# Projection steps of a hybrid S5 / delta-rule encoder given to the scheduler with high priority

## The chip, the cores and the metric

The kernel runs on one core of one Trainium2 chip. The metric is the device time of one execution in microseconds, the median of three runs.

## What is computed

One encoder block in float32 on a sequence of 512 tokens of width 1024. The input is normalized and projected by `w_in` to a stream u for an S5 scan (width 512), to q, k, v, z for a gated delta rule with 4 heads of 128 (512 each), and to the gates beta and a. Cut to what matters:

```
h = rmsnorm(x); u, q, k, v, z, beta, a = split(h @ w_in)
y = s5_scan(u, forward) + s5_scan(u, backward)          # 32 groups of 16 channels, 64 states
q, k, v = silu(conv5(q, k, v)); q, k = l2norm(q), l2norm(k)
o = chunked_delta(q, k, v, g, beta) + flip(chunked_delta(flipped))   # chunks of 64
mix = concat(s5 output, norm(o) * silu(z)) @ w_out + x
x2 = mix + cross_attention(mix, mem)                     # memory of 256 rows
out = x2 + mixture_of_experts(x2)                        # 4 x 8 experts, 2 chosen
```

## The kernel before

`build` (L1510 on) issues the work stage by stage in Python. A scheduler then lists the instructions of each engine: it runs a timeline of its own and takes, of those that are ready, the one with the highest priority, by default the one that was issued first. On the chip every engine works through its list strictly in order. So the order in which `build` issues steps, and any priority that it gives them, set the lists.

The stages around the change, in the order of the program:

- `stage_a` normalizes and transposes x into `ht` (8 blocks of 128 by 512 tokens). `proj_u` makes four projections by `proj` (L179: one 512 KB weight load `wst` through SP's queue, four buffers, then eight matmuls of 128x512 in `mm8`, L143, into one of two banks). `gates` makes the decays; it ends with nine small copies on DVE (L579 to L598: gc, sdl, sbe, csr, cso), between which ACT loads a table for exp (L580).
- `gdn_in` (L614) makes the 12 blocks k0, q0, k1, q1, ..., k3, q3, v0 to v3. Each: a projection, two copies out of its bank by ACT (xp L636, cv L637), two small memsets of xp on POOL (L633, L634), four taps on DVE (L639), silu on ACT (L640), four transposes (L648); for q and k also squares, a power on POOL (L666), a scaling and four more transposes (L673). Its pool reuses the memory of the gates, so the first xp waits for the last of the gates' copies.
- `s5_params` (L232 on) makes the S5 tables in eight steps. Each makes `pm` and `ca` by a complex multiply of six 128x512 operations (L225 to L230) on DVE or POOL, by two lists of eight entries (`PM_ENG`, `CA_ENG`), writes `ca` to memory, transposes `pm` (L372), copies it (`bct`, L373), multiplies `bb` by `ca` (L381), copies the result (`wl`, L387 on), writes it to `w_scr`, and multiplies `bct` by the transposed u (L404). `pm`, `ca` and `bct` have one buffer each.
- `weave` advances several generators in turn in proportion to given counts; here it interleaves the 13 steps of `gdn_in` with the 9 of `s5_params` (L1556).
- Next, woven again: `gdn_inv` (the matrix N of the delta rule in four blocks, L698 to L726, a series of 31 steps on DVE, its products L768 to L778), four z projections and eight memory blocks `mem_kv` (128x256 matmuls, also L143), and the recurrence `s5_rec` on DVE. Then `gdn_chain` (eight dependent steps, PE at L834 to L851) with the other eight memory blocks; then the output of the S5 scan (`tz`, L446, read back from `w_scr`), the mixing, the cross attention, and the experts, whose weights stream in to the end.

Of the kernel before, what the change touches and what calls it, by code (L numbers as in the profile page):

```python
# [43 lines left out]
def weave(*streams):  # L44

    live = [[g, n, 0] for g, n in streams]
    while live:
        s = min(live, key=lambda t: (t[2] + 0.5) / t[1])
        s[2] += 1
        if next(s[0], s) is s:  # L50
            live.remove(s)


CA_ENG = (1, 1, 0, 1, 1, 1, 0, 1)
# [3 lines left out]
class Enc:  # L58
# [1448 lines left out]
    def build(self):  # L1507
        nc, tc, ctx, A = self.nc, self.tc, self.ctx, self.A
# [40 lines left out]
        with tc.tile_pool(name="gi", bufs=2) as gi:  # L1549
            qkv = self.gdn_in([(w, n, h) for h in range(4) for w, n in ((1, "k"), (0, "q"))] +  # L1550
                              [(2, "v", h) for h in range(4)], gi)
            s5 = self.s5_params()
            next(s5)
            for _ in u:
                pass
            weave((qkv, 13), (s5, 9))  # L1556

        self.gp2 = pool(left, "gp2")
        self.gp3 = pool(left, "gp3")
# [7 lines left out]

        inv = self.gdn_inv()
        weave((inv, 16), (rest(), 13), (itertools.islice(rec, 16), 17))
        gv.close()  # L1570
        r2.close()
        self.set_banks(ch=(3, 4, 5, 6, 7), out=(2,), tp=(1,), mm=(0,))
        weave((self.gdn_chain(), 20), (kv, 9), (rec, 47))
        r1.close()

# [202 lines left out]
```

## Time and profile before

| | us |
|---|---|
| three runs | 893.8, 893.03, 889.67 (median 893.03) |
| the profiled execution | 892.26 |
| its span | 890.5 |
| PE busy | 783.1 (88%) |
| DVE busy | 404.3 (45%) |
| ACT busy | 329.4 (37%) |
| POOL busy | 232.6 (26%) |

PE is TensorE's matmuls, PEld its weight loads, DVE VectorE, ACT ScalarE, POOL GpSimd, SP SyncE, whose queue carries most of the transfers. Start times count from the start of the span. A matmul of 128x512 in float32 shows as two records. PEclk is the granted TensorE clock as a share of full speed, so 0.50 is the lower of its two levels (1.2 GHz) and 1.00 the upper (2.4 GHz). A bracket at the end of a row is the idle time of the engine ahead of it, and what ended it.

### The profile page before, as it was taken

What the parts mean: (1) busy time and instruction counts of PE and PEld (TensorE: products, weight loads), DVE (VectorE), ACT (ScalarE), POOL (GpSimd) and SP (SyncE); (2) the same over time, 40 slices, a digit from 0 to 9 for tenths busy, and PEclk for the clock granted to TensorE, in tenths of its full rate; (3) what the DMA queues carried; (4) which work ended last, traced back from release to release, by engine and by line L of the source; (5) the groups of instructions that cost most, each with busy time, mean ns of one, the idle gap of its engine ahead of it and who ended that gap; (6) DMA issues with size and microseconds to landing.
All of it is one profiled execution on the core that took longest, in us unless ns stands there. A gap on an engine that the chain in (4) does not pass through costs nothing. (4 is left out here: it accounts for less than half of the span.)

```text
span 890.5 us, 12981 instructions
## 1 busy us (share of the span) xinstructions
PE 783.1 (88%) x4735; PEld 492.2 (55%) x4736; DVE 404.3 (45%) x1044; ACT 329.4 (37%) x760; POOL 232.6 (26%) x237
## 2 busy tenths in 40 slices
PE   5986998998997997899899999996698878788983
PEld 3443554555586875676688879895333333333331
DVE  4288767678899522244643554324210000000375
ACT  4242454455413235465343464333232131312204
POOL 1022857832100111205161332241311011100103
PEclk9996998999997998999999999998799999999997
DMA  7837222322663308615663714595699999999982
GB/s 206 144 91 111 74 78 74 100 76 98 225 193 104 108 24 169 116 56 172 184 224 96 260 49 159 194 406 187 248 391 412 414 411 408 395 391 410 410 350 102
DMA packets 128130, 185.17 MB, mean 208 GB/s; under 512 B 38734, under 2 KB 93006, under 8 KB 123968
## 3 DMA queue, kind: packets, MB, share of 16 engines
q1 hardware_dynamic: 122736, 172.31, 57.6%
q0 software_dynamic: 5328, 12.01, 3.6%
q8 instruction: 38, 0.62, 0.3%
q14 instruction: 28, 0.23, 0.1%
HBM read 165.50 MB, written 26.18 MB: 215 GB/s over the span
## 5 line engine op out<-in xcount | busy, mean ns | idle before, releaser
L143 PE MATMUL bank<-ht,wst 128*128 128x512 f32 x320 | 151.3, 621 | 4.2 <-ACT kd L583 2.4
L1340 PE MATMUL bank<-mw,xt 128*64 128x512 f32 x360 | 104.5, 595 | 1.5 <-DMA mw<-in_moe_w_up_dram 1.5
L143 PEld LDWEIGHTS bank<-ht,wst 128*128 128x128 f32 x320 | 60.7, 198 | 73.4 <-issue 68.3
L1344 DVE SCALAR_TENSOR_TENSOR hs<-hs,tw,bank 128x256 f32<-128x256 f32 x16 | 7.7, 480 | 168.9 <-ACT hs L1343 168.9
L1343 ACT ACTIVATE hs<-bank,tw 128x256 f32<-128x256 f32 x16 | 7.6, 474 | 155.5 <-PE bank L1340 155.5
L1380 PE MATMUL bank<-mw,hT 128*64 128x512 f32 x152 | 50.6, 660 | 16.2 <-ACT yd L1385 16.2
L1340 PEld LDWEIGHTS bank<-mw,xt 128*64 128x64 f32 x360 | 33.5, 138 | 55.6 <-issue 52.4
L143 PE MATMUL bank<-mt,wst 128*128 128x256 f32 x256 | 59.9, 393 | 0.0
L639 DVE SCALAR_TENSOR_TENSOR cv<-xp,taps,cv 128x512 f32<-128x512 f32 x48 | 50.4, 1049 | 20.8 <-ACT cv L637 19.7
L972 POOL TENSOR_TENSOR wlo<-wst,whi 128x1024 fp32r<-128x1024 f32 x16 | 38.6, 2416 | 78.7 <-ACT whi L971 78.7
L143 PEld LDWEIGHTS bank<-mt,wst 128*128 128x128 f32 x256 | 50.0, 198 | 7.7 <-issue 0.6
L1320 POOL DMA_INDIRECT xg<-t_scr,tidx x16 | 16.5, 1029 | 136.4 <-PE bank L1327 133.4
L824 POOL TENSOR_TENSOR kt<-kn,kd 64x512 f32<-64x512 f32 x14 | 14.5, 1035 | 97.6 <-PE bank L778 49.8
L1330 ACT ACTIVATE xt<-bank,gm 128x128 f32<-128x128 f32 x128 | 34.7, 382 | 8.9 <-PE bank L1327 7.8
L149 PE MATMUL bank<-wlo,oh 128*128 128x256 f32 x128 | 36.6, 289 | 0.0
L854 DVE SCALAR_TENSOR_TENSOR S<-S,egl,bank 128x128 f32<-128x128 f32 x48 | 15.5, 345 | 46.1 <-PE bank L851 46.1
L150 PE MATMUL bank<-whi,oh 128*128 128x256 f32 x128 | 35.8, 283 | 0.0
L1380 PEld LDWEIGHTS bank<-mw,hT 128*64 128x64 f32 x152 | 14.0, 148 | 38.7 <-issue 20.8
L151 PE MATMUL bank<-whi,ol 128*128 128x256 f32 x128 | 35.3, 287 | 0.0
L149 PE MATMUL bank<-mlo,mxh 128*128 128x512 f32 x64 | 25.8, 405 | 0.8 <-DVE gss L484 0.8
L903 POOL TENSOR_TENSOR mlo<-mst,mhi 128x512 fp32r<-128x512 f32 x16 | 22.0, 1393 | 14.8 <-ACT mhi L902 14.2
L150 PE MATMUL bank<-mhi,mxh 128*128 128x512 f32 x64 | 25.7, 402 | 0.0
(551 smaller groups left out, 1826.3 us busy)
## 6 DMA issues: line engine op xcount, KB each, us to landing
mw<-in_moe_w_down_dram SPq DMA_DIRECT2D x23, 1024.0 KB, 14.7
mw<-in_moe_w_gate_dram SPq DMA_DIRECT2D x45, 512.0 KB, 8.3
mw<-in_moe_w_up_dram SPq DMA_DIRECT2D x45, 512.0 KB, 13.9
wst<-in_w_in_dram SPq DMA_DIRECT2D x20, 512.0 KB, 4.5
ca_scr<-ca SPq DMA_DIRECT2D x8, 512.0 KB, 2.7
wst<-in_xa_wk_dram SPq DMA_DIRECT2D x8, 512.0 KB, 4.3
y_scr<-lhc SPq DMA_DIRECT2D x2, 2048.0 KB
wst<-in_xa_wv_dram SPq DMA_DIRECT2D x8, 512.0 KB, 4.3
```

Of the source, the lines that this page charges most:

```text
L143: self.nc.tensor.matmul(ps, w[:, k, :], act[:, k, :], start=(k == 0), stop=(k == 7))
L149: self.nc.tensor.matmul(ps, ah, bl, start=(first and i == 0), stop=False)
L150: self.nc.tensor.matmul(ps, ah, bh, start=False, stop=False)
L151: self.nc.tensor.matmul(ps, al, bh, start=False, stop=(last and i == n - 1))
L639: v.scalar_tensor_tensor(cv, xp[:, w:w + T], taps[:, w, m:m + 1], cv, op0=OP.mult, op1=OP.add)
L854: v.scalar_tensor_tensor(sn, S[di, h], self.egl[:, ch % 2, ch // 2, di * 4 + h:di * 4 + h + 1], p, op0=OP.mult, op1=OP.add)
L903: nc.gpsimd.tensor_tensor(lo[:, k], st, hi[:, k].bitcast(F32), op=OP.subtract)
L972: nc.gpsimd.tensor_tensor(lo, st, hi.bitcast(F32), op=OP.subtract)
L1320: self.gather = g_.indirect_dma_start(out=xg, out_offset=None, in_=self.t_scr, in_offset=bass.IndirectOffsetOnAxis(ap=self.tidx[:, q:q + 1 ...
L1330: nc.scalar.activation(xt[:, k], ps[:, (k % 4) * P:(k % 4 + 1) * P], AF.Copy, scale=self.gm[:, k:k + 1])
L1340: nc.tensor.matmul(pg[w * 64:w * 64 + 64].rearrange("p (a n) -> p a n", a=2), xt[:, k, w * 64:w * 64 + 64], un[k // 4 * 2 + w][:, :, k % 4 ...
L1380: nc.tensor.matmul(py[w * 64:w * 64 + 64], hT[:, k, w * 64:w * 64 + 64], wd[w][:, k, c], start=(k == 0), stop=(k == 1))
```

## The change

A generator `ahead` passes on the steps of another one, each inside the scheduler's high priority; `build` wraps `gdn_in` in it. Everything below moves down by nine lines. Nothing is computed otherwise than before.

```diff
+def ahead(tc, g):
+
+    while True:
+        with tc.high_priority():
+            if next(g, g) is g:
+                return
+        yield
...
-            weave((qkv, 13), (s5, 9))
+            weave((ahead(tc, qkv), 13), (s5, 9))
```

The lists of the engines change by this. Three places:

**PE, from the last matmul of the gates to the first S5 table.** Banks 571 and 585 are the last two u projections, 607 is k0, 715 q0, 832 k1; `pm` is the first table. Before:

```order
L578 MATMUL bank_280<-g,hfm 128x32 x2
L125 MATMUL bank_357<-ident,U 128x128 x2
L143 MATMUL bank_585<-ht,wst 128x512 x2
L143 MATMUL bank_607<-ht,wst 128x512 x8
L125 MATMUL bank_365<-ident,U 128x128 x2
L143 MATMUL bank_715<-ht,wst 128x512 x2
L125 MATMUL bank_353<-ident,U 128x128 x2
L143 MATMUL bank_715<-ht,wst 128x512 x3
L372 MATMUL bank_656<-ident,pm 128x128 x4
L372 MATMUL bank_662<-ident,pm 128x128 x4
```

Now:

```order
L152 MATMUL bank_607<-ht,wst 128x512 x8
L587 MATMUL bank_280<-g,hfm 128x32
L134 MATMUL bank_357<-ident,U 128x128 x2
L152 MATMUL bank_585<-ht,wst 128x512 x2
L381 MATMUL bank_656<-ident,pm 128x128 x4
L381 MATMUL bank_662<-ident,pm 128x128 x4
L390 MATMUL bank_686<-ca,bb 32x128
L134 MATMUL bank_365<-ident,U 128x128 x2
L390 MATMUL bank_686<-ca,bb 32x128 x5
L134 MATMUL bank_353<-ident,U 128x128 x2
L390 MATMUL bank_686<-ca,bb 32x128 x2
L152 MATMUL bank_832<-ht,wst 128x512 x8
```

k0 still stands ahead of the first table; the five matmuls of q0 that did now stand behind it, and behind the eight of k1 (832), which come first.

**DVE, at the end of the gates.** `b` is an input of `pm`; P are the partial products. Before:

```order
L579 COPY gc<-bank_280 128x32
L228 TENSOR_TENSOR b_392<-b_392,d_560 128x512
L230 TENSOR_TENSOR b_392<-b_392,d_561 128x512
L582 TENSOR_TENSOR sdl<-bank_280,gc 128x32
L589 SCALAR_TENSOR_TENSOR sbe<-beta,egc 128x16
L594 TENSOR_SCALAR csr<-egc 64x4x4
L597 COPY cso<-egc 64x4x4
```

Now:

```order
L357 MEMSET dd 128x128
L234 TENSOR_TENSOR P_637<-aF,b_392 128x512
L235 TENSOR_TENSOR P_638<-aF,b_392 128x512
L236 TENSOR_TENSOR pm<-aF,b_392 128x512
L238 TENSOR_TENSOR pm<-aF,b_392 128x512
L359 TENSOR_TENSOR dd<-ident,dT 16x128 x4
L237 TENSOR_TENSOR pm<-pm,P_637 128x512
L239 TENSOR_TENSOR pm<-pm,P_638 128x512
L234 TENSOR_TENSOR P_754<-aF,b_392 128x512
L235 TENSOR_TENSOR P_755<-aF,b_392 128x512
L588 COPY gc<-bank_280 128x32
L591 TENSOR_TENSOR sdl<-bank_280,gc 128x32
```

The first `pm` and two products of the second now stand ahead of the gates' copies, which stood ahead of it.

**PE, at the first two of the four blocks of N.** Banks 1750 and 1817 hold their differences, 1771 and 1838 the products of k and q; 1801, 1868, 1935 and 2006 are the z projections, 1641 and 1660 belong to tables. Before:

```order
L716 MATMUL bank_1771<-kT 64x64
L717 MATMUL bank_1771<-qT,kT 64x64
L143 MATMUL bank_1801<-ht,wst 128x512 x8
L703 MATMUL bank_1817<-lef,g 64x64 x8
L703 MATMUL bank_1817<-geb,g 64x64 x7
L648 MATMUL bank_1719<-ident,cv 128x128 x4
```

Now, ahead of the first block, and between the first and the second:

```order
L390 MATMUL bank_1660<-ca,bb 32x128 x2
L152 MATMUL bank_1935<-ht,wst 128x512 x6
L152 MATMUL bank_2006<-ht,wst 128x512 x3
L413 MATMUL bank_1641<-uperm,bct 64x64 x14
L712 MATMUL bank_1750<-lef,g 64x64 x8
L712 MATMUL bank_1750<-geb,g 64x64 x8
```

```order
L725 MATMUL bank_1771<-kT 64x64
L726 MATMUL bank_1771<-qT,kT 64x64
L712 MATMUL bank_1817<-lef,g 64x64 x8
L712 MATMUL bank_1817<-geb,g 64x64 x8
L725 MATMUL bank_1838<-kT 64x64
L726 MATMUL bank_1838<-qT,kT 64x64
```

Before, one z projection of eight matmuls stood behind each block of N. Now 27 of their 32 matmuls stand ahead of the first block, four in the third, and one behind the last. The memory blocks behind them move up: 11 instead of 9 stand ahead of the products of the series (L768 before), 12 are done by the first step of the chain where 11 were, and when the last is done 5 steps of the chain are, where 7 were.

## Rows read from the trace of the kernel before

**Rows 1.** Busy time by stretch. Columns: the stretch in us and its length; then busy us (and instructions) of PE, PEld, DVE, ACT and POOL; the granted clock PEclk; the busy share of the DMA engines; GB/s.

```profile
67.44:74.84 7.40, 0.01 (x1) 0.03 (x1) 7.28 (x11) 2.82 (x4) 5.61 (x8) 0.78 1.39 101
74.84:82.80 7.96, 7.96 (x31) 4.25 (x32) 7.89 (x15) 1.97 (x4) 0.14 (x2) 0.50 0.57 141
143.72:154.50 10.78, 10.78 (x35) 4.42 (x36) 9.09 (x12) 5.69 (x18) 6.28 (x7) 0.70 0.13 50
202.53:245.57 43.04, 40.59 (x334) 23.42 (x334) 37.07 (x142) 21.41 (x27) 9.10 (x5) 0.96 0.49 169
245.57:280.68 35.11, 29.30 (x136) 25.49 (x135) 35.03 (x153) 3.08 (x9) 1.28 (x1) 0.99 0.62 185
280.68:301.82 21.14, 21.14 (x293) 19.11 (x294) 16.08 (x54) 9.72 (x18) 4.10 (x4) 0.70 0.18 53
301.82:331.10 29.28, 28.97 (x186) 23.70 (x185) 8.13 (x34) 9.27 (x31) 2.07 (x2) 1.00 0.19 59
400.00:616.30 216.30, 211.06 (x1245) 175.82 (x1244) 89.59 (x168) 92.34 (x179) 69.49 (x46) 0.99 0.57 199
641.50:890.40 248.90, 205.76 (x936) 81.60 (x936) 49.38 (x82) 63.76 (x191) 38.58 (x42) 0.95 0.94 373
```

**Rows 2.** The timeline of PE, from the last projections ahead of the tables. Columns: start in us, busy us of the group, engine, line, operation, out<-in, tile, shape, type, records, and in brackets the idle time ahead of it with what ended it.

```profile
62.66 1.98 PE L143 MATMUL bank<-ht,wst 128*128 128x512 f32 x4 [2.35 <-ACT kd L583]
64.70 2.74 PE L143 MATMUL bank<-ht,wst 128*128 128x512 f32 x6
74.84 1.94 PE L372 MATMUL bank<-ident,pm 128*128 128x128 f32 x8 [7.39 <-DVE pm L228]
78.46 0.69 PE L125 MATMUL bank<-ident,U 128*128 128x128 f32 x2
79.09 1.08 PE L381 MATMUL bank<-ca,bb 64*32 64x128 f32 x10
...
143.72 0.63 PE L381 MATMUL bank<-ca,bb 64*32 64x128 f32 x2 [4.03 <-POOL xp L634]
```

**Rows 3.** The timeline of DVE at the same place, same columns.

```profile
59.90 0.18 DVE L579 COPY gc<-bank 128x32 f32<-128x32 f32 x1
...
60.60 0.68 DVE L230 TENSOR_TENSOR b<-b,d 128x512 f32<-128x512 f32 x1
...
66.24 0.69 DVE L225 TENSOR_TENSOR P<-aF,b 128x512 f32<-128x512 f32 x1
...
67.45 0.34 DVE L593 COPY csr<-sbe 64x16 f32<-64x16 f32 x2
...
68.44 1.75 DVE L229 TENSOR_TENSOR pm<-aF,b 128x512 f32<-128x512 f32 x1
70.11 3.86 DVE L350 TENSOR_TENSOR dd<-ident,dT 16x128 f32<-16x128 f32 x4
74.00 0.69 DVE L228 TENSOR_TENSOR pm<-pm,P 128x512 f32<-128x512 f32 x1
```

**Rows 4.** The timeline of POOL at the same place: the first and the second half of the first `ca`.

```profile
61.58 1.11 POOL L225 TENSOR_TENSOR P<-aR,ct 128x512 f32<-128x512 f32 x1 [5.45 <-issue]
...
68.07 1.57 POOL L228 TENSOR_TENSOR ca<-ca,P 128x512 f32<-128x512 f32 x1
```

**Rows 5.** The timeline of ACT at the same place: the table load of the gates, and the copies out of k0's bank.

```profile
60.15 1.28 ACT L580 ACT_TABLE_LOAD   x1 [4.61 <-DVE gc L579]
...
68.75 0.68 ACT L637 ACTIVATE cv<-bank,taps 128x512 f32<-128x512 f32 x1
```

**Rows 6.** The timeline of PE from the blocks of N to the products of the series.

```profile
202.53 0.68 PE L703 MATMUL bank<-lef,g 128*64 128x64 f32 x16
...
236.66 7.13 PE L143 MATMUL bank<-ht,wst 128*128 128x512 f32 x16
243.63 31.24 PE L143 MATMUL bank<-mt,wst 128*128 128x256 f32 x144
280.68 6.82 PE L768 MATMUL bank<-XT,N 32*32 32x32 f32 x128 [5.81 <-issue]
...
296.67 5.31 PE L143 MATMUL bank<-mt,wst 128*128 128x256 f32 x16
```

**Rows 7.** The timeline of DVE at the last block of N and at the start of the series.

```profile
239.91 0.68 DVE L707 TENSOR_TENSOR e<-bank,gc 128x512 f32<-128x512 f32 x1
...
243.23 1.62 DVE L720 SCALAR_TENSOR_TENSOR N<-bank,beta,e 128x64 f32<-128x64 f32 x8 [1.20 <-ACT e L710]
244.77 0.74 DVE L724 TENSOR_TENSOR qkd<-bank,e 128x256 f32<-128x256 f32 x2
...
245.57 1.97 DVE L731 STREAM_TRANSPOSE NT<-N 128x1024 f32<-128x1024 f32 x1
```

**Rows 8.** The timeline of PE in the chain: its first step, two products of one late step and the next, and the first product of the S5 output.

```profile
301.82 0.38 PE L840 MATMUL bank<-vc,lhc 128*128 128x128 f32 x2
...
333.18 0.49 PE L840 MATMUL bank<-r,lhc 128*128 128x128 f32 x2
...
335.38 0.49 PE L840 MATMUL bank<-r,lhc 128*128 128x128 f32 x2
...
347.45 0.66 PE L446 MATMUL bank<-tz,uperm 128*64 128x128 f32 x2 [4.67 <-DMA tz<-w_scr]
```

**Rows 9.** The page's list of DMA issues: KB each, and the median us from issue to landing.

```profile
wst<-in_w_in_dram SPq DMA_DIRECT2D x20, 512.0 KB, 4.5
```

## The prediction

> **What bounds the kernel now.** I read the page's busy shares first, then the busy time by stretch, then the timelines of PE and of the engines that it waits for. PE is the most used engine, and by stretch two regimes are to be seen. From 641.5 us on, the transfers of the experts' weights bind: their share is 0.94, while PE is busy 205.8 of 248.9 us. From 400 to 616 us PE is busy 211 of 216 us [rows 1]. Ahead of the experts PE is the bound, so time saved on PE before 400 us passes to the end one for one, because the routing, and with it the experts' weights, starts that much earlier. What can be saved is PE's idle time and what it runs at the lower clock. Around the change the timeline of PE shows three such places: 2.35 and 7.39 us ahead of the first table, the second of them put down to DVE's `pm`; 4.03 us ahead of a `ca` product at 143.72 us [rows 2]; 5.81 us at the end of the series [rows 6]. After the first of them the granted clock is 0.50 from 74.84 to 82.80, after the second it is 0.70 over 10.78 us [rows 1].
>
> A second limit lies in the series of 31 steps: DVE is busy 35.03 of 35.11 us there, and PE fills it with 9 memory blocks (144 records) and then waits [rows 1, 6]. Work that is put ahead of the N blocks delays that series; work that is kept for it is hidden.
>
> **The change, part by part.** The arithmetic stays, so each term is a move. The sum runs to the first product of the S5 output, and what follows is taken as unchanged.
>
> *The start.* Before, the gates' copies stood on DVE between `b` (done at 61.28) and the first product P (66.24); the useful `pm` was done at 74.69 and PE went on at 74.84 [rows 2, 3]. Now P follows `b`. Five multiplies and the four `dd` stand ahead of PE. Where POOL is idle a multiply takes 0.69; beside POOL's `ca` one took 1.75, and the four `dd` 3.86 [rows 3, 4]. All at 0.69: 61.3 + 3.5 + 3.9 = 68.6; all at 1.75: 61.3 + 8.75 + 3.86 = 73.9. POOL starts `ca` at 61.58 and had 5.45 us of waiting ahead of it [rows 4], so only the first P is ahead of it: 61.3 + 0.69 + 7.0 + 3.86 = 72.8, and I take that. So the first table is 2 us earlier, not 5.
>
> The Trainium skill, page "SBUF — State Buffer", section "Who interferes with whom", says that a DVE instruction with two SBUF inputs contends with a GpSimd instruction that reads SBUF, and that the port pair they share is an exclusive lock. The trace agrees in kind (0.69 against 1.75). By that rule each of the eight operations after the first would last at least one of POOL's 1.57, `pm` would come at 61.3 + 0.69 + 12.6 = 74.6, and the sum below would be worse by 1.8.
>
> The price is paid behind it. The gates' copies now come after `pm`, its second half and two more products: 72.8 + 3 x 0.69 = 74.9. xp of k0 waits for the last of them, and k1 (bank 832) on PE waits for k0's copies. From gc to the end of cv took 59.90 to 69.43, 9.5 us, with copies that ran beside POOL; alone it is 1.5 to the end of the table load, eight copies of 0.18 and two ACT copies of 0.68 [rows 3, 5]: about 4.5. POOL has done its eight products by then (61.58 + 8 x 1.57 = 74.1), so I take 5: k1 starts at 79.9. PE's table work in between (74.84 to 80.17 before [rows 2]) fits in. Before, PE at 80.17 already had five matmuls of q0 behind it (the ten records at 62.66 and 64.70), at 7.13/8 = 0.89 each 4.5 us [rows 2, 6], and two pairs of transposes at 0.69 more. So PE is 4.5 + 1.4 - 0.3 = **5.6 us behind**. Ends: 68.6 + 2.1 + 4.5 = 75.2 gives 0.9; 73.9 + 3 x 1.75 + 9.5 = 88.7 gives 14.4. The clock is 0.50 after the wait in either order.
>
> *The tables' waits.* The wait of 4.03 at 143.72, with the 0.60 x 10.78 us at half rate that followed (3.2 us lost), falls away, since projections that stood behind that table now stand ahead: **-7.2**. In return the projections run out sooner, and later tables stand on PE with less cover, in order, behind `ca` and `pm` of POOL. What that costs no row shows: between nothing, and two waits like the one of before (14.4). I take **+5**, between one such wait without its loss of clock (4.0) and one with it (7.2).
>
> Weight loads keep up: one lands in 4.5 us [rows 9] with four buffers and a block takes 7.13, so a load that is held behind a late `ca_scr` write on SP's queue has 21 us of cover. POOL's xp memsets are tiny and only move with the taps. I count both at nothing.
>
> *Arrival at N.* 27 matmuls of the z projections now stand ahead of it: 27 x 0.89 = 24.1. The first difference (202.53 [rows 6]) moves to 202.5 + 24.1 + 5.6 - 7.2 + 5 = 230.0.
>
> *The N blocks.* They took 43.04 us with four z projections between them (28.5 of PE). Now only their own rounds are left. One round, from e (239.91) to the start of the series (245.57), takes 5.66, with ACT's table load and exp inside it [rows 7]; four in a row 22.6; DVE's own part alone 4 x (0.68 + 1.62 + 0.74) = 12.2. Since N waited for ACT's e even with a projection for cover, I take 22: the series starts at 252.0, **6.4 later** than at 245.57. It lasts as long (35.1), and PE has two memory blocks more to fill it: products at 287.1 instead of 280.68.
>
> *To the chain.* The 21.14 us between hold two memory blocks now and PE is busy in all of them [rows 1]; one block (5.31 [rows 6]) is gone: 15.8, so the chain starts at 302.9 instead of 301.82, with 12 blocks done instead of 11. Then 4 blocks and 5 steps, instead of 5 and 7 in 29.28 us: less 31.24/9 = 3.5 and 2 x 2.2 (333.18 to 335.38 [rows 8]) = 21.4. The memory blocks end at 324.3 instead of 331.10: -6.8. The read of `tz` from `w_scr`, for which PE waits 4.67 us, follows them [rows 8]. The two chain steps are owed later, +4.4. Net **-2.4**.
>
> *Sum.* 892.26 - 2.4 = 889.9; the profiled execution lies 0.8 below the median of 893.03. I say 890.0. About 0.5% (4.5 us) is what a measurement of this kernel can tell from no change.
>
> **The rivals.** *The tables are never late (0.26).* The +5 is nothing: 884.9. For it: PE had to wait only once for POOL in eight tables. Against it: then it had a projection between each two.
>
> *The tables bind, slower (0.26).* POOL and DVE hold each other up at their complex multiplies, and with the projections gone ahead, PE stands at a `ca` or `pm` in order, loses the clock, and runs the next matmuls at 0.50 as after 74.84. With two such waits, 14.4 instead of 5: 889.9 + 9.4 = 899.3. It decides from 7.4 us of new waiting on. For it: the 4.03 us at 143.72 end on POOL, and the multiply of 1.75 beside it. Against it: z projections now stand among the last tables as cover. The skill's rule on the shared port, told above, speaks for this case.
>
> *Nothing moves where it counts (0.06).* The lists change, but the S5 output waits for the same read of `tz`, and the chain for the same steps: what is won at 324 is waited away at 347. 892.
>
> **How the numbers follow.** Forecast 0.42, within 3 us of 890.0. The range has to reach to both rivals: 884.9 less some of the start's low end, and 899.3 with some of its high end: 881 to 901. Faster by over 0.5% (under 888.6): the first rival and 0.12 of the forecast, 0.38. Slower (over 897.5): 0.23 of the second and 0.03 of the forecast's tail, 0.26. The rest, 0.36, is within 0.5%.
>
> **What would show it.** PE waits once ahead of the first table for about 13 us, until 72 to 75, and again ahead of k1 until about 80; no wait for POOL at q and k blocks; the first N difference near 230 and the series near 252; products near 287; the chain's first step near 303; the last memory block near 324. It is wrong if PE stands for more than 8 us in all at table products after 85 us, if the N rounds take far less than 5.5 us each, or if the S5 output starts no earlier than 347 although the memory blocks end early.

## The result, and the profile after

The changed kernel takes 886.17 us in the median (16 runs, 881.87 to 888.8), the kernel before 891.81 in the same series (16 runs, 887.1 to 894.95): the ratio is 0.9938, 95% interval 0.992 to 0.9957, so 5.5 us faster. The forecast's sum gave 2.4 us.

The profiled execution, the fastest of the 16, has a span of 880.1 us, 10.4 less than before, which is more than the medians differ by. Part of it is not of the change: the first matmul of the gates, ahead of everything that moves, starts at 47.90 where it started at 49.95. Below, places are therefore counted from that matmul, and two traces of each kernel are used.

Busy time by stretch, with the columns of [rows 1]: the wait ahead of the first table, the matmuls after it, the N blocks, the series, the products, chain and memory blocks, and the last 250 us.

```profile
58.04:71.12 13.08, 0.00 (x0) 0.03 (x1) 12.76 (x13) 0.00 (x0) 10.88 (x8) 0.65 0.26 81
71.12:82.30 11.18, 11.18 (x35) 5.81 (x36) 9.66 (x26) 6.43 (x11) 0.20 (x4) 0.50 0.35 83
222.21:246.83 24.62, 20.63 (x308) 16.34 (x305) 19.11 (x74) 11.21 (x15) 4.92 (x4) 1.00 0.52 172
246.83:282.05 35.22, 31.42 (x146) 26.73 (x144) 35.14 (x154) 3.85 (x10) 1.27 (x1) 1.00 0.61 179
282.05:296.88 14.83, 14.83 (x275) 13.71 (x276) 11.81 (x44) 8.98 (x16) 1.03 (x1) 0.77 0.08 24
296.88:319.40 22.52, 22.21 (x138) 18.18 (x136) 20.17 (x84) 7.43 (x25) 5.15 (x5) 1.00 0.20 59
630.00:880.00 250.00, 205.85 (x942) 80.53 (x938) 49.45 (x82) 63.88 (x191) 38.69 (x42) 0.96 0.94 373
```

The N blocks take 24.6 us instead of 43.0, the series as long as before, the stretch to the chain 14.8 instead of 21.1, and the tail has the busy shares of [rows 1]. From the router's first matmul to the end it took 277.0 and 277.8 us in two traces of before, 278.1 and 279.4 in two of the change, so what PE saves ahead of it reaches the end but for about 1 us.

The timeline of PE, as in [rows 2, 6, 8]:

```profile
71.12 1.94 PE L381 MATMUL bank<-ident,pm 128*128 128x128 f32 x8 [13.08 <-DVE pm L237]
75.81 1.05 PE L390 MATMUL bank<-ca,bb 64*32 64x128 f32 x4
76.79 16.75 PE L152 MATMUL bank<-ht,wst 128*128 128x512 f32 x32
...
171.37 7.13 PE L152 MATMUL bank<-ht,wst 128*128 128x512 f32 x16 [1.61 <-ACT cv L646]
...
222.21 0.64 PE L712 MATMUL bank<-lef,g 128*64 128x64 f32 x16
...
282.05 5.70 PE L777 MATMUL bank<-XT,N 32*32 32x32 f32 x128 [2.75 <-DVE XT L758]
...
296.88 0.38 PE L849 MATMUL bank<-vc,lhc 128*128 128x128 f32 x2
...
319.40 0.44 PE L967 MATMUL bank<-ident,kvo 128*128 128x128 f32 x2
...
335.80 0.66 PE L455 MATMUL bank<-tz,uperm 128*64 128x128 f32 x2 [2.17 <-issue]
```

One long wait stands at the start. Behind it PE waits for no table at all: between 72 and 222 us only two waits are left, both for a copy by ACT, the larger of them 1.61 us. The 4.03 us at 143 are gone.

The timeline of DVE at the start, as in [rows 3]:

```profile
59.46 0.63 DVE L234 TENSOR_TENSOR P<-aF,b 128x512 f32<-128x512 f32 x1
60.01 1.58 DVE L235 TENSOR_TENSOR P<-aF,b 128x512 f32<-128x512 f32 x1
61.51 1.58 DVE L236 TENSOR_TENSOR pm<-aF,b 128x512 f32<-128x512 f32 x1
63.02 1.58 DVE L238 TENSOR_TENSOR pm<-aF,b 128x512 f32<-128x512 f32 x1
64.53 4.83 DVE L359 TENSOR_TENSOR dd<-ident,dT 16x128 f32<-16x128 f32 x4
69.39 1.48 DVE L237 TENSOR_TENSOR pm<-pm,P 128x512 f32<-128x512 f32 x1
...
72.59 0.18 DVE L588 COPY gc<-bank 128x32 f32<-128x32 f32 x1
...
75.14 0.18 DVE L607 COPY cso<-egc 64x16 f32<-64x16 f32 x1
```

And POOL beside it, as in [rows 4]:

```profile
59.44 1.60 POOL L234 TENSOR_TENSOR P<-aR,ct 128x512 f32<-128x512 f32 x1 [5.35 <-issue]
...
64.02 1.55 POOL L238 TENSOR_TENSOR ca<-aR,ct 128x512 f32<-128x512 f32 x1
65.53 1.30 POOL L237 TENSOR_TENSOR ca<-ca,P 128x512 f32<-128x512 f32 x1
...
69.17 1.14 POOL L235 TENSOR_TENSOR P<-aR,ct 128x512 f32<-128x512 f32 x1
```

The first P takes 0.63 us although POOL's first product starts with it (that one takes 1.60). The other four multiplies beside POOL take 1.48 to 1.58, and the four `dd` 4.83 together. The gates' small operations (eleven by the trace, not nine), with POOL idle, need 2.7 us in all.

### The profile page after: what moved, and what is told of

The parts are those of the page before. It is cut to its first block, busy times and chain, and to the rows that moved or that the text cites. A ratio compares the mean times of both kernels' runs of the same rounds, so it can differ in the third digit from the quotient of the medians.

```text
span 880.1 us, 12961 instructions
## 1 busy us (share of the span) xinstructions
PE 776.8 (88%) x4735; PEld 485.7 (55%) x4736; DVE 399.7 (45%) x1044; ACT 324.9 (37%) x755; POOL 233.4 (27%) x237
## 5 line engine op out<-in xcount | busy, mean ns | idle before, releaser
L152 PE MATMUL bank<-ht,wst 128*128 128x512 f32 x320 | 147.2, 612 | 4.0 <-issue 2.2
L863 DVE SCALAR_TENSOR_TENSOR S<-S,egl,bank 128x128 f32<-128x128 f32 x48 | 15.2, 344 | 34.0 <-PE bank L860 33.7
L160 PE MATMUL bank<-mhi,mxl 128*128 128x512 f32 x64 | 25.9, 407 | 0.9 <-DVE mxl L926 0.9
```

What stands on the lines that cost most here:

```text
L152: self.nc.tensor.matmul(ps, w[:, k, :], act[:, k, :], start=(k == 0), stop=(k == 7))
L160: self.nc.tensor.matmul(ps, al, bh, start=False, stop=(last and i == n - 1))
L863: v.scalar_tensor_tensor(sn, S[di, h], self.egl[:, ch % 2, ch // 2, di * 4 + h:di * 4 + h + 1], p, op0=OP.mult, op1=OP.add)
```

## The experiments

Since the experiments move the same work to other places, a landmark that comes earlier is no gain by itself. So I kept a ledger of PE from the gates' first matmul to the router (613.44 us in the trace of before), where the tail begins: idle time, and time lost to the clock (busy time times one minus the granted clock, summed over pieces of 3 us). Idle time is given to the first table, from there to the first difference of N, and from there to the router. All in us, each from one trace; the ratio is that of the timed runs.

| kernel | idle to table | to N | to router | clock | gates to router | ratio |
|---|---|---|---|---|---|---|
| before | 9.7 | 5.7 | 22.5 | 21.5 | 563.5 | 1 |
| before, again | 8.1 | 5.8 | 23.6 | 19.8 | 561.3 | |
| the change | 13.1 | 2.0 | 20.2 | 14.4 | 554.1 | 0.9938 |
| the change, again | 13.1 | 2.0 | 17.8 | 21.3 | 557.2 | |
| from k1 on | 9.8 | 2.4 | 17.4 | 19.3 | 549.2 | 0.9853 |
| from k2 on | 8.1 | 1.3 | 16.7 | 22.1 | 549.6 | 0.9872 |
| v only | 9.8 | 4.6 | 16.9 | 19.1 | 554.2 | 0.9947 |
| k0, q0 only | 13.1 | 2.6 | 22.1 | 17.5 | 557.8 | 0.9961 |
| k and q only | 13.1 | 5.6 | 23.1 | 21.7 | 568.4 | 1.0061 |
| change, z held back | 13.1 | 9.5 | 21.5 | 22.3 | 571.8 | 1.0115 |
| before, z first | 8.1 | 5.7 | 22.9 | 30.8 | 575.6 | 1.0118 |
| change, dd early | 9.1 | 7.7 | 22.1 | 20.8 | 563.2 | 1.0026 |
| from k1 on, dd early | 8.4 | 2.8 | 16.8 | 21.0 | 547.9 | 0.9869 |

In the mean of the two traces of each kernel, PE's way from the gates to the router is 6.7 us shorter with the change: 3.6 us of it are idle time, 2.8 are clock. But the two traces of the change differ by 6.9 us in the clock and by 2.4 in the idle time behind N, so how the gain divides between the two is not settled.

**The change, again.** The same kernel.

> The changed kernel once more, for a second trace of it. The first pair of traces differs by 10.4 us of span, the medians by 5.6. If the 2.05 us that PE already stood apart at the gates' first matmul (49.95 before, 47.90 after), ahead of anything that the change moves, is scatter of one execution, that matmul comes anywhere between 47.5 and 50.5 here, and the distance from it to the first difference of N (174.3 us in the first trace) and to the first product of the S5 output (287.9) stays within 1 us. Rival: those distances scatter by 3 us too, and then the trace pair can't be read to better than that.

The gates' first matmul came at 49.04, the waits up to the S5 output came again to a few tenths, and the first difference of N lay 172.8 us behind that matmul (174.3), but the first product of the S5 output 290.6 (287.9). Both distances miss the 1 us that I allowed. So the waits are of the kernel, and the distances scatter by up to 3 us, as the rival says. Most of that lies in the clock. Busy time of this second trace, from the products of the series to the chain:

```profile
281.64:299.96 18.32, 18.32 (x274) 16.67 (x275) 13.04 (x46) 8.98 (x16) 2.34 (x3) 0.60 0.11 33
```

The same matmuls (one record fewer falls into the window here), behind the same wait of 2.75 us, took 14.83 us at a granted clock of 0.77 in the first trace and 18.32 at 0.60 here.

**Before, again.** The same kernel with nine empty lines.

> The kernel before once more (nine empty lines put in, so that its lines have the numbers of the changed kernel), for a second trace. Its waits of PE should come again to 0.3 us each (7.39, 4.03, 2.45, 5.81, 4.67, 3.30), its time at the lower clock should differ from the first trace's 21 us by some microseconds, as that of the two traces of the changed kernel did (14 and 21). Rival: the waits themselves scatter, and then the comparison wait by wait says nothing.

```profile
72.78 1.94 PE L381 MATMUL bank<-ident,pm 128*128 128x128 f32 x8 [5.69 <-DVE pm L237]
...
140.80 0.63 PE L390 MATMUL bank<-ca,bb 64*32 64x128 f32 x2 [4.03 <-POOL xp L643]
...
344.02 0.66 PE L455 MATMUL bank<-tz,uperm 128*64 128x128 f32 x2 [4.75 <-DMA tz<-w_scr]
```

Four of the six waits come again to 0.1 us. Two miss the 0.3 that I expected, 5.69 for 7.39 and 7.23 for 5.81. For the first of them the places agree all the same (the table comes 24.9 us behind the gates' matmul in both): the busy time of the matmuls ahead differs instead, whose ends are modelled. The clock's loss differs by 1.7 us here. The two pairs of traces together give 562.4 us before and 555.7 after, 6.7 less, against 5.5 by the runs, which include the tail.

**From k1 on.** The start alone is undone.

```diff
 def ahead(tc, g):
+    n = 0
     while True:
-        with tc.high_priority():
-            if next(g, g) is g:
-                return
+        if n >= 2:
+            with tc.high_priority():
+                if next(g, g) is g:
+                    return
+        elif next(g, g) is g:
+            return
+        n += 1
         yield
```

> High priority from the third block (k1) on only: k0 and q0 keep their place, so PE has q0's five matmuls ahead of the first table and the gates' copies stand ahead of pm as before; the order from there to the N blocks is that of the changed kernel. My theory: the start cost the changed kernel 4.6 us on PE, and that is paid one for one at the end: 5.6 + 4.6 = 10 us faster than before, ratio about 0.989, first difference of N some 4.6 us earlier after the gates' first matmul than in the changed kernel (about 169.7 us behind it). Rival: the late start is made up anyway, because the tables then meet operands that are ready; ratio 0.994 as the changed kernel, distance about 174.

0.9853 (0.9822 to 0.9884), 877.01 us: faster than both kernels. The first N difference comes 166.0 us behind the gates' matmul, 7.5 earlier than in the change, with the same 930 records of PE ahead of it in both. My theory's direction holds and its size was too small. The timeline of PE at the first table:

```profile
73.37 1.94 PE L385 MATMUL bank<-ident,pm 128*128 128x128 f32 x8 [7.39 <-DVE pm L241]
```

The start is that of before and the waits for tables are as rare as in the change (2.4 us). 3.3 us of the difference are idle time at the start. The rest is busy time, 153.9 us up to N against 159.2 and 157.7 in the two traces of the change. The largest part of it is in the `ca` products, 11.7 us against 15.2 in both; what is left is of the size by which the two traces of the change differ. Why those products take less here no run shows.

**k0 and q0 only.** The complement, `if n < 2`.

> High priority for k0 and q0 only: the start is that of the changed kernel (first table ahead of q0's matmuls, the gates' copies behind pm), and the z projections stand between the N blocks as before. My theory, after the kernel with priority from k1 on gained 13 us where the full change gained 5.5: the start alone costs some 7 us of PE's time (3.3 us more of idle, the rest at the lower clock): ratio 1.005 to 1.009. Rival: a late start is absorbed where PE waits for the tables anyway (4.03 us at 143 us): ratio 1.000, and that wait is gone from the trace.

0.9961 (0.9941 to 0.9981): faster, so my theory that the start alone costs 7 us falls, and the rival holds, even beyond its number. The start's wait is there:

```profile
72.31 1.94 PE L385 MATMUL bank<-ident,pm 128*128 128x128 f32 x8 [13.09 <-DVE pm L241]
...
176.06 0.66 PE L394 MATMUL bank<-ca,bb 64*32 64x128 f32 x14 [0.45 <-DVE ca L243]
```

but the wait of 4.03 is gone and so is that of 2.45 ahead of v3's transposes; behind the first table the largest wait up to the N blocks is 1.33 us. Costs of places in the list don't add. Here PE, being later, found ready what it had waited for at 143 us, and the late start cost nothing in the end. In the full change, where that wait is gone anyway, undoing the late start brought 7.5 us.

**k and q only**, `if n < 8`: the v blocks and three of the four z projections stay where they were; one moves ahead of N.

> High priority for the k and q blocks only: the start is that of the changed kernel, but the v blocks stay among the last tables and the four z projections stand between the N blocks as before. My theory: without the z part only what was won up to the first difference of N is left, 2.4 us by the traces: ratio about 0.997 (between 0.994 and 1.000). Rival: all of the gain is the wait for POOL at 143 us and its loss of clock, the N blocks and what follows are neutral: ratio 0.994 as the changed kernel.

1.0061 (1.003 to 1.0093), slower than before; both expectations are missed. With the start of the change, waits for tables are as long as before, elsewhere:

```profile
71.69 1.94 PE L385 MATMUL bank<-ident,pm 128*128 128x128 f32 x8 [13.08 <-DVE pm L241]
...
189.72 0.48 PE L417 MATMUL bank<-uperm,bct 128*64 128x64 f32 x4 [4.12 <-ACT bct L386]
```

**v only**, `if n >= 8`.

> High priority for the four v blocks only: the start and the k and q blocks are those of the kernel before; two of the four z projections move ahead of the N blocks among the last tables. My theory now: what gains is that PE has other matmuls to run wherever a table is late, so it gains the waits from 160 us on (1.08 + 0.35 + 2.45 us of idle and some clock) but keeps the 4.03 us at 143: ratio 0.993 to 0.997. Rival: the k and q blocks ahead are what counts and v's place is neutral: ratio 1.000.

0.9947 (0.9922 to 0.9971): as my theory says, and within the intervals all of the change's gain. The wait at 143 stays, the later ones are gone:

```profile
142.53 0.63 PE L394 MATMUL bank<-ca,bb 64*32 64x128 f32 x2 [4.04 <-POOL xp L647]
...
275.06 5.13 PE L781 MATMUL bank<-XT,N 32*32 32x32 f32 x102 [3.35 <-issue]
```

**From k2 on**, `if n >= 4`.

> High priority from the fifth block (k2) on: k0, q0, k1 and q1 keep the places of the kernel before. If the 13 us of the kernel with priority from k1 on come from the start left alone and from cover for the last tables, k1 and q1 don't matter: ratio 0.985 to 0.989. If each block that goes ahead adds its share, it lies halfway to the kernel with v alone (0.9947): 0.990.

0.9872 (0.984 to 0.9904), not to be told from the kernel with priority from k1 on, so no gain of k1 and q1 is shown. k2 to q3 do gain, against v alone: the wait of 4.04 at 143, which v alone leaves, is gone here, and idle time from the first table to N is 1.3 us instead of 4.6.

**The change with z held back.** The z projections take bank 7, which the last table uses to its end.

```diff
-        ps = self.ps("mm")
+        ps = self.ps(bank)
...
-            ps = self.proj(2048 + h * P)
+            ps = self.proj(2048 + h * P, "zb")
...
-        self.set_banks(mm=(0, 1), tp=(2,), iv=(4, 5, 6, 7))
+        self.set_banks(mm=(0, 1), tp=(2,), iv=(4, 5, 6, 3), zb=(7,))
```

> The full change, but the four z projections take the bank that the last table uses to the end, so that none can start ahead of the N blocks (the N blocks get bank 3 instead of it): all 12 projections stay ahead, z stands between the N blocks as in the kernel before. If what gains is that z's matmuls run where the last tables are late, PE now idles there: more than 10 us of new idle time between the first table and the first N difference, and a time above the kernel before, ratio 1.005 to 1.02. If z only changed places with the N blocks, that difference comes 24 us earlier (about 149 us behind the gates' first matmul), PE idles no more than in the changed kernel, and the ratio stays about 0.994.

1.0115 (1.0087 to 1.0143): 1.8% above the change, and slower than before. PE now waits in front of the last tables:

```profile
194.46 1.03 PE L413 MATMUL bank<-uperm,bct 128*64 128x64 f32 x28 [0.81 <-ACT bct L382]
...
202.22 0.63 PE L390 MATMUL bank<-ca,bb 64*32 64x128 f32 x2 [6.72 <-POOL ca L237]
```

Idle time up to N is 9.5 us instead of 2.0 (7.5 more, where I expected over 10), and the first N difference comes 159.5 us behind the gates' matmul, 14 us ahead of the change instead of 24: 10 of the 24 us of z's matmuls had cost nothing, because the tables were not ready. This is my second rival of the prediction, tables that bind with no cover, and the z projections are what keeps it from coming. The edit also gives z one bank instead of two and the N blocks another fourth bank. The N blocks took 45.2 us here, against 43.0 in the kernel before, so some 2 us of the loss may come from that; the 7.5 us ahead of N don't.

**Before, with z first.** No priority; the z projections are issued ahead of the N blocks.

```diff
-        def rest():
-            yield from self.proj_z()
-            yield from itertools.islice(kv, 8)
+        for _ in self.proj_z():
+            pass
+
+        def rest():
+            yield from itertools.islice(kv, 8)
...
-        weave((inv, 16), (rest(), 13), (itertools.islice(rec, 16), 17))
+        weave((inv, 16), (rest(), 9), (itertools.islice(rec, 16), 17))
```

> The kernel before, no priority, but with the four z projections issued ahead of the N blocks instead of woven between them. My theory: the N blocks without projections between them take about 25 us instead of 43, the series starts about 6 us later than before, the memory blocks end about 5 to 7 us earlier, and most of this stays: ratio 0.992 to 0.996. Rival: it is the same work in another order, PE is as full as before: ratio 1.000, or slower by the 6 us by which the series starts later (1.006).

1.0118 (1.008 to 1.0156): my theory falls. z's last matmuls end at 229.3, 24.7 us ahead of the series, where it said about 25. Counted from the gates' matmul, the memory blocks end 9.3 us earlier (5 to 7 expected) and the S5 output starts 10.2 earlier. But the series starts 9.9 later (6 expected) and the chain 9.5, and the chain's outputs are then owed:

```profile
335.82 0.66 PE L446 MATMUL bank<-tz,uperm 128*64 128x128 f32 x2 [3.20 <-issue]
...
445.90 1.11 PE L882 MATMUL bank<-ident,ot 128*128 128x128 f32 x4 [2.03 <-DVE ot L879]
```

From the gate product of the S5 output to the router PE is busy 225.9 us instead of 209.8, and 9.0 us instead of 1.7 go to the clock. So z ahead of N alone does not gain in this form, and landmarks that come earlier prove nothing. But this edit moved the memory blocks too: two were left for the chain, where the kernel before has five and the change four. That it is z among the tables which gains rests on the kernel with z held back, not on this one.

**The change with dd early.** The four multiplies stand behind the copy of their input `dT`.

```diff
                 v.tensor_copy(dT, ps[:16, 64:96])
+                dd = tq.tile([P, 8, 16], F32, name="dd")
+                v.memset(dd, 0.0)
+                for cg in range(4):
+                    v.tensor_tensor(dd[cg * 32:cg * 32 + 16], self.ident[:16, None, :16].to_broadcast([16, 8, 16]),
+                                    dT[:, cg * 8:(cg + 1) * 8, None].to_broadcast([16, 8, 16]), op=OP.mult)
...
-                dd = tl.tile([P, 8, 16], F32, name="dd")
-                v.memset(dd, 0.0)
-                for cg in range(4):
-                    v.tensor_tensor(dd[cg * 32:cg * 32 + 16], self.ident[:16, None, :16].to_broadcast([16, 8, 16]),
-                                    dT[:, cg * 8:(cg + 1) * 8, None].to_broadcast([16, 8, 16]), op=OP.mult)
```

> The full change, and the four dd multiplies on DVE made right behind their input, at about 35 us, instead of between the first table's multiplies beside POOL (4.83 us there). My theory: the start's wait is bound by DVE's chain to the first pm, so PE's wait of 13.08 us falls by 4 to 5 us and the end comes as much earlier against the changed kernel: ratio to before about 0.989. Rival: PE then stands 4 us longer behind the gates' copies ahead of the next projection, and nothing is won: 0.994.

1.0026 (1.0004 to 1.0049): slower than the change. The first wait falls by 4.0 us as expected, and others take its place, as the rival says. (Ahead of the gates' first matmul, where the ledger does not yet count, PE waits 1.00 us instead of 0.26 in both kernels with `dd` early.)

```profile
69.28 1.09 PE L381 MATMUL bank<-ident,pm 128*128 128x128 f32 x4 [9.12 <-DVE pm L237]
70.75 1.12 PE L381 MATMUL bank<-ident,pm 128*128 128x128 f32 x4 [0.38 <-DVE pm L239]
75.87 0.69 PE L134 MATMUL bank<-ident,U 128*128 128x128 f32 x2 [2.81 <-ACT egl L593]
...
128.37 1.98 PE L152 MATMUL bank<-ht,wst 128*128 128x512 f32 x4 [2.52 <-ACT cv L646]
```

2.81 us go to the gates' copies at once; the other waits come from a list that was laid anew behind it. It lost more than the rival allowed.

**From k1 on, with dd early.** The same edit on the fastest kernel, whose list of PE stays but for a few records.

> Priority from k1 on, with the dd multiplies made early. The lists of PE are those of the kernel with priority from k1 on. My theory: its wait of 7.39 us ahead of the first table falls by 3.9 to about 3.5, the clock stays up longer, and the time comes to about 0.980 of before (873). Rival: the first ca on POOL, or the gates' copies, take its place: 0.985 as without.

0.9869 (0.9839 to 0.99), not to be told from without. The two waits ahead of the first table go from 2.36 and 7.39 to

```profile
63.18 1.98 PE L156 MATMUL bank<-ht,wst 128*128 128x512 f32 x4 [3.81 <-ACT kd L596]
72.55 1.09 PE L385 MATMUL bank<-ident,pm 128*128 128x128 f32 x4 [4.59 <-DVE pm L241]
...
222.53 6.27 PE L156 MATMUL bank<-ht,wst 128*128 128x512 f32 x7 [3.64 <-issue]
```

so 1.35 of 3.9 us are won: the first of them, for the gates' exponentials on ACT, grew. Among the N blocks a wait of 1.90 us ahead of z's last matmuls became the 3.64 shown. Again the rival holds.

## Why the prediction came out as it did

The time lay in the range of 881 to 901 and the sign was right. The size was half of what came: 886.17 lies outside the 3 us around 890.0, in the case "faster by over 0.5%" that had a chance of 0.38. Step by step, counted from the gates' first matmul where a place is meant (before: 49.95):

- **The start: right, in part by luck.** The first table was forecast for 72.8, 22.9 us behind that matmul; it came at 23.2 in both traces. One multiply at full speed and four slowed by POOL, as the sum had it, but the four took 6.2 us instead of 7.0 and `dd` 4.83 instead of 3.86: two errors that cancel. The row of before that is nearest in its surroundings, not the fastest, was the price to take. The Trainium skill's rule of the shared port pair (page "SBUF — State Buffer", section "Who interferes with whom") would have put it 1.8 us later, by the estimate there. The trace agrees with the rule and not with that working: from the second multiply on, DVE ends one operation to each of POOL's, the multiplies of 1.58 beside POOL's 1.55 and the four `dd`, 1.2 each, beside POOL's 1.30 to 1.14. What was too long is the 1.57 for each of POOL's operations. The late start's price at N, forecast at 5.6 us, was 7.5 by the kernel with priority from k1 on.
- **k1 at 79.9: nearly right, for another reason.** 76.79 is 28.9 behind the matmul, 30.0 were forecast. The gates' copies were not what it waited for: cv of k0 was done at 76.3 and PE was still at the table.
- **The wait at 143 gone, -7.2: right.** 4.03 us and its loss of clock are gone (the granted clock is 1.00 on the average from 82.30 to N); so are 1.5 us of smaller waits (0.24, 1.08 and 0.20) that I had not counted.
- **New waits for tables, +5: they did not come.** PE idles 2.0 us between the first table and N in both traces, none of it for `ca` or `pm`: its two waits, 0.24 and 1.61, are ahead of projections, for a copy by ACT. This was my first rival's case. What I had not priced is the cover: the 27 matmuls of z that I added as a delay of N were the ones that ran while the last tables were late. Holding them back brought 7.5 us of idle time and 1.8% of the time; so the second rival is real, and what decides between it and the first here is z's place.
- **N: first difference 6.5 us too late in the forecast, series 3.9 us.** 173.5 us behind the matmul in the mean of two traces against 180.1; the series at 198.2 against 202.1. The N blocks took 24.6 us, not 22: PE waited 2.17 us ahead of the z matmuls left among them, and 1.82 ahead of a memory block, for a copy of z by ACT.
- **Series: right. Memory blocks, S5 output: right in number, in part by luck.** The series lasted 35.2 us. The memory blocks ended 7.3 us earlier than before in the mean of two traces each (6.8 forecast), the S5 output 7.6. But N had come 6.5 us earlier than forecast. The longer N blocks took back 2.6 of that, and the stretch from the chain's first step to the last memory block 1.8 more: it shrank by 6.1 us in the mean, from 27.8 to 21.4 and 22.1, where 7.9 were forecast.
- **The two chain steps owed, +4.4: mis-sized.** From the first product of the S5 output to the router it took 266.0 and 265.1 us before, and 266.2 and 266.7 after: 0.9 more in the mean. Two things were wrong in the term. It took the spacing of two steps' starts for their price, and it had all of them owed at the S5 output. By then PE had caught up on part of them: 20 records more than before stood behind that product (1694 against 1674), and PE's busy time on the chain (L834 to L851 before) ahead of it was 19.2 us instead of 21.3, so 2.0 us were owed. And against them PE's idle time from there to the router fell by 1.9 us in the mean (8.7 and 8.5 before, 7.9 and 5.5 after); the clock cost some 1 us more, which is within its scatter. So 3.5 of the 4.4 us were not paid, and that is about what the forecast was short of.

## What to carry to other kernels

In this kernel, work without a deadline (z) was worth most where the engine would have waited for something slow, so a priority is judged by which filler it leaves beside which late producer. Landmarks that come earlier prove nothing while the same work is only owed later; compare idle time plus time at the lower clock up to a common point. Undo a change by blocks: here leaving two of the twelve blocks out of the priority more than doubled the gain.

## What was not expected of the hardware

Two traces of one kernel, with the same lists and, up to the S5 output, the same waits within some tenths, lost 14.4 and 21.3 us to the lower clock. Behind the same idle stretch of 13.08 us the granted clock was still 0.50 from 78 to 81 us in the first (1.2 GHz), and 0.77 on the average of 79 to 82 in the second, where the wait had ended 1.15 us later. Busy time in these two pieces:

```profile
78.00:81.00 3.00, 3.00 (x5) 1.16 (x4) 3.00 (x7) 1.84 (x3) 0.00 (x0) 0.50 0.33 111
```

```profile
79.00:82.00 3.00, 3.00 (x7) 1.38 (x6) 3.00 (x7) 1.99 (x3) 0.00 (x0) 0.77 0.37 121
```

Five records in the one and seven in the other. Here the first trace was the slower one. Its smaller total comes from later places, as the stretch from the products of the series to the chain shown above (14.83 us at 0.77 against 18.32 at 0.60). Differences of some microseconds between two single executions of this kernel are of this kind, and say nothing of a change.
